# First FFN product of a hybrid decoder layer: a second pair of places for the raw weights of odd units, and shared places for three other tiles

## The chip, the cores and the metric

The kernel runs on one core of one Trainium2 chip. The metric is the time of one launch in microseconds (us), of which the median of several runs is given. One core has five engines that work side by side, each through its own list of instructions in order: TensorE (PE, matmuls, with weight loads shown apart as PEld), VectorE (DVE), ScalarE (ACT), GpSimd (POOL) and SyncE (SP, which only issues transfers). They wait for each other by semaphores. On-chip working memory is divided into tiles of 128 partitions; results of PE appear in banks of 128x512 fp32 numbers, which DVE or ACT then read.

## The reference, cut to what matters

```
h    = rms_norm(x, norm_mix_g)                    # x: 1024 x 1024
proj = h @ w_in                                   # then two attentions, gated and merged
x    = x + merged @ w_out
h2   = rms_norm(x, norm_ffn_g)                    # 1024 x 1024
gu   = h2 @ w_ffn_in                              # 1024 x 5632: gate g and up u, 2816 columns each
x    = x + (silu(gu[..., :2816]) * gu[..., 2816:]) @ w_ffn_down
return rms_norm(x, norm_final_g)
```

All is fp32. The change concerns the line `gu = h2 @ w_ffn_in` with the gate silu(g) * u.

## The kernel before, in words

**Numbers.** A product of two fp32 operands is made of three matmuls. Each operand is held as a pair: a high part (`wh` for weights, `hi` in the code), which ACT makes by a copy in a reduced format (L96), and a low part (`wl`, `lo`), which DVE makes by subtracting the high part from the original (L97). PE multiplies high by high, high by low and low by high.

**Units.** The columns of `w_ffn_in` are worked in 22 units j of 128 columns of g and 128 columns of u. Units 0 and 1 are made plainly (`plain`, in the pool "first"). Units 2 to 21 are made by `up` in the pool "up", with a Winograd form of Strassen's scheme over the pair (g, u) and the two halves of the inner dimension: seven products of half the size instead of eight. Each is 12 matmuls (four blocks of the inner dimension, three matmuls each), 84 in a unit. The left sides come from the raw weights of the unit, two transfers of 512 KB (g and u) that SP issues in `raw_w` (L251) into places named "wr":

- A1: the raw g, split by ACT and DVE.
- S12: u1 + u2 (POOL, L272) and that less g1 (POOL, L273), then split.
- S34: g1 - u1 (L276) and g2 less the second half of S12 (L277), then split.
- A22: u2, the second half of the raw u, split.

In the trace these tiles are all `wh` and `wl`; the raw place is `wr`, the sums are `s`. The right sides (T1 to T4, B11 to B22) are made once, before, and are `hT_t` and `tT` in the trace.

The two raw places of "wr" in the general pool `wpool` are shared by all units, one for g and one for u: the next unit's g can be loaded only when A1, L273, L276 and L277 of this unit have read it.

**Banks and gates.** Each unit takes three of six banks, b1, b2, b3; so a unit's b1 is the b1 of two units before. ACT copies b1 to c1 (L1046), DVE adds (`from_bank`, shown as L978) b2 and c1 to v2; after a second product in b1, ACT takes its sigmoid into sg1 (L1054), and DVE multiplies b1 into sg1 (L978, `sg<-pd,sg`: the last reader of b1). DVE makes v3 (b2 + c1), a2 (b3 + v3) and a1 (b2 + c1); POOL multiplies a1 by sg1 (L1062, the first gate multiply). After the unit's last product DVE makes gt2 (b3 + v2, `gt<-pd,v`), ACT its sigmoid sg2 (L1065), POOL gt2 by sg2 (L1066) and a2 by sg2 (L1067, the second gate multiply). c1, v2, v3, sg1, sg2 and gt2 have one place each in the pool "up"; `a` has two.

**Pairs of units.** The first eight pairs, (2,3) to (16,17), go on into another Strassen scheme for the next product, so each pair's results are combined by four DVE operations into `f1` (L1071, `left_rows`), which are run during the unit after the pair; in the code `todo` carries them there:

```
            vi = from_bank(v2[:], b2, c1)
            if todo:
                with tc.issue_after(vi.ins):
                    left_rows(*todo)
```

POOL's queue then stores `f1` (L1081), and each unit's `a` is stored by POOL's queue too (L1089, L1091, L1094).

**What sets the order.** The order of the instructions on each engine is set at build time by a scheduler that plans with estimated durations and with the places (a new tile of a name waits until the old one in its place has been read); `issue_after` holds an operation back behind another. So a change of places changes the order, too. In the steady order PE runs, from the start of unit n on: A1[:4] x B11 into b1 of n (the start of unit n); A22 x T4 into b2 of n-2; S34[4:] x B22 into b3 of n-2 (the last product of n-2); S12[4:] x T2 into b2 of n; A1[4:] x B21 into b1 of n-1; S12[:4] x T1 into b3 of n and S34[:4] x T3 into b2 of n-1 in turns; then the start of unit n+1. POOL runs in a unit L272 and L273 (of the unit that starts next), L1062, L1066, and then L276, L277, L1067, or, where it has DMAs of a pair to issue, L1067, L276, L277 and the DMAs.

**Around the stage.** Ahead of it lie units 0 and 1, whose last store to `a_dram` (L1007) is in SP's queue ahead of the first loads of the stage. Behind it the next product begins with loads of rows of `a_dram` (L119) into the same raw places of `wpool`.

Of the kernel before, what the change touches and what calls it, by code (L numbers as in the profile page):

```python
# [8 lines left out]
F32 = mybir.dt.float32  # L9
# [6 lines left out]
P = 128  # L16
D = 1024
S = 1024
KT = D // P
# [10 lines left out]
DFF = 2816  # L30
# [17 lines left out]
def layer_kernel(  # L48
# [18 lines left out]
    w_out, w_ffn_in, w_ffn_down = w_out[0], w_ffn_in[0], w_ffn_down[0]  # L67

    def pool_of(name, bufs, side="left"):
        return tc.tile_pool(name=name, bufs=bufs, side=side, reuse_waits="tile")  # L70


    wpool = ctx.enter_context(tc.tile_pool(name="wpool", bufs=2))
# [14 lines left out]
    def nm(s):  # L88
        uid[0] += 1
        return f"{s}_{uid[0]}"  # L90

    def pd():
        return psd.tile([P, HALF], F32, tag="d", name=nm("pd"))

    def split(hi, lo, src):
        nc.scalar.activation(out=hi, in_=src, func=AF.Copy)  # L96
        return nc.vector.tensor_tensor(out=lo, in0=src, in1=hi.bitcast(F32), op=ALU.subtract)  # L97
# [148 lines left out]
    B11, B21 = hT[0][:, :4], hT[0][:, 4:]  # L246
    B12, B22 = hT[1][:, :4], hT[1][:, 4:]

    def raw_w(src):
        t = wpool.tile([P, KT, P], F32, tag="wr", name=nm("wr"), bufs=2)  # L250
        last_w[0] = nc.sync.dma_start(out=t[:], in_=src.rearrange("(k p) c -> p k c", p=P))  # L251
        return t

    def pair_of(raw):

        w = Pair(*[wpool.tile([P, KT, P], F32R, tag="w" + n, name=nm("w" + n), bufs=2) for n in "hl"])
        split(w.hi[:], w.lo[:], raw)
        return w

    def left_side(pool, rg, ru, bufs):  # L260

        def pair(k, tag, bufs):
            return Pair(*[pool.tile([P, k, P], F32R, tag=tag + n, name=nm("w" + n), bufs=bufs) for n in "hl"])

        def fill(w, raw):
            split(w.hi[:], w.lo[:], raw)
            return w

        g1, g2, u1, u2 = rg[:, :4], rg[:, 4:], ru[:, :4], ru[:, 4:]
        S34, A22, A1 = pair(KT, "s34", 1), pair(4, "a22", 2), pair_of(rg[:])  # L270
        s12 = pool.tile([P, KT, P], F32, tag="s", name=nm("s12"), bufs=2)
        nc.gpsimd.tensor_tensor(out=s12[:, :4], in0=u1, in1=u2, op=ALU.add)  # L272
        nc.gpsimd.tensor_tensor(out=s12[:, 4:], in0=s12[:, :4], in1=g1, op=ALU.subtract)  # L273
        S12 = fill(pair(KT, "s12", bufs), s12[:])
        s34 = pool.tile([P, KT, P], F32, tag="s", name=nm("s34"), bufs=2)
        nc.gpsimd.tensor_tensor(out=s34[:, :4], in0=g1, in1=u1, op=ALU.subtract)  # L276
        nc.gpsimd.tensor_tensor(out=s34[:, 4:], in0=g2, in1=s12[:, 4:], op=ALU.subtract)  # L277
        return A1, S12, fill(S34, s34[:]), fill(A22, u2)

    def prod(bank, a, b, first=False):  # L280
        for k in range(4):
            w, m = a[:, k], b[:, k]
            for n, (p, q) in enumerate(((w.hi, m.hi), (w.hi, m.lo), (w.lo, m.hi))):
                last_mm[0] = nc.tensor.matmul(bank[:], p, q, start=first and k == 0 and n == 0,  # L284
                                              stop=k == 3 and n == 2, skip_group_check=True)

    def projections(pool, T, c, dst, dls, sc, hl=False):
# [16 lines left out]

        cc, v2, v3 = [pool.tile([P, HALF], F32, tag=n, name=nm(n), bufs=1) for n in ("cc", "v2", "v3")]
        A1, S12, S34, A22 = left_side(pool, *[raw_w(w_in[:, c0:c0 + P]) for c0 in c], 1)
        b1, b2, b3 = pd(), pd(), pd()

# [73 lines left out]
    with pool_of("foxv", 2) as vpool:  # L382
# [31 lines left out]
        for i in range(NT):  # L414
            load_x()
            hh, c = divmod(i * P, HALF)
# [137 lines left out]
    fpool = f_ctx.__enter__()  # L554
# [288 lines left out]
    for i, (br, dt) in enumerate(merge_order):  # L843
        n = br * KT + dt
# [62 lines left out]
    def rows_of(d):  # L907
        return d.rearrange("n p c -> p n c")
# [5 lines left out]
    with pool_of("wout", 2) as mpool:  # L914
# [13 lines left out]
        for c0 in range(0, D, HALF):  # L928
            ws = []
            for hh in range(2):  # L930
# [12 lines left out]
                if hh == 0:  # L943
                    for k in range(KT):
                        if k % 2 == 0:
                            src = w_out[k * P:(k + 2) * P, c0:c0 + HALF]
# [30 lines left out]
    def from_bank(out, bank, other, op=ALU.add):  # L977
        return nc.vector.tensor_tensor(out=out, in0=bank[:], in1=other[:], op=op)  # L978
# [5 lines left out]
    with pool_of("first", 2) as fpool:  # L984
# [26 lines left out]
        def vec(out, p, q, op=ALU.subtract):  # L1011
            nc.vector.tensor_tensor(out=out[:], in0=p[:], in1=q[:], op=op)
# [21 lines left out]
    with pool_of("up", 1) as fpool:  # L1034

        def tmp(n):
            return fpool.tile([P, HALF], F32, tag=n, name=nm(n), bufs=1)

        def up(j, todo):
            A1, S12, S34, A22 = left_side(fpool, *[raw_w(w_ffn_in[:, c:c + P]) for c in (j * P, DFF + j * P)], 2)  # L1040
            b1, b2, b3 = pd(), pd(), pd()
            a = fpool.tile([P, S], F32, tag="a", name=nm("a"), bufs=2)
            a1, a2 = a[:, :HALF], a[:, HALF:]
            c1, v2, v3, sg1, sg2, gt2 = [tmp(n) for n in ("c1", "v2", "v3", "sg1", "sg2", "gt2")]
            prod(b1, A1[:, :4], B11, True)
            nc.scalar.activation(out=c1[:], in_=b1[:], func=AF.Copy)  # L1046
            prod(b2, S12[:, 4:], T2, True)
# [4 lines that stand above are left out]
            prod(b1, A1[:, 4:], B21)  # L1052

            nc.scalar.activation(out=sg1[:], in_=b1[:], func=AF.Sigmoid)  # L1054
            from_bank(sg1[:], b1, sg1, ALU.mult)
            prod(b2, S34[:, :4], T3)
            from_bank(v3[:], b2, c1)
            prod(b3, S12[:, :4], T1, True)
            from_bank(a2, b3, v3)
            prod(b2, A22, T4)  # L1060
            from_bank(a1, b2, c1)
            nc.gpsimd.tensor_tensor(out=a1, in0=a1, in1=sg1[:], op=ALU.mult)  # L1062
            prod(b3, S34[:, 4:], B22)
            from_bank(gt2[:], b3, v2)
            nc.scalar.activation(out=sg2[:], in_=gt2[:], func=AF.Sigmoid)  # L1065
            nc.gpsimd.tensor_tensor(out=sg2[:], in0=gt2[:], in1=sg2[:], op=ALU.mult)  # L1066
            nc.gpsimd.tensor_tensor(out=a2, in0=a2, in1=sg2[:], op=ALU.mult)  # L1067
            return a[:].rearrange("p (b c) -> p b c", b=2)

        def vec(out, p, q, op=ALU.subtract):  # L1070
            nc.vector.tensor_tensor(out=out, in0=p, in1=q, op=op)  # L1071
            return out

        def left_rows(n, p, q):

            s = f1
            vec(s[:, 0], p[:, 1], q[:, 1], ALU.add)
            vec(s[:, 1], s[:, 0], p[:, 0])
            vec(s[:, 2], p[:, 0], p[:, 1])
            vec(s[:, 3], q[:, 0], s[:, 1])  # L1080
            nc.gpsimd.dma_start(out=rows_of(left_dram[n, 3:7]), in_=s[:])  # L1081

        todo, one = None, None
        for j in range(PLAIN, NFF):
            n, second = divmod(j - 2, 2)
            a = up(j, todo)
            todo = None
            if n >= len(TWO_ROWS):
                nc.gpsimd.dma_start(out=a_dram[j], in_=a.rearrange("p b c -> p (b c)"))  # L1089
            elif second:  # L1090
                nc.gpsimd.dma_start(out=rows_of(left_dram[n, 1:3]), in_=a)  # L1091
                todo = (n, one, a)
            else:
                nc.gpsimd.dma_start(out=left_dram[n, 0], in_=a[:, 0])  # L1094
                one = a
# [5 lines left out]
    with pool_of("down", 1) as fpool:  # L1101
# [79 lines left out]
        A11, A12, A22, S1, S2, S3, S4 = range(7)  # L1181
# [71 lines left out]
```

## Time and profile before

| | us |
|---|---|
| median of 3 runs | 1499.15 |
| lowest and highest | 1495.67, 1503.45 |
| the profiled execution's own time | 1500.5 |
| its span in the profile | 1498.7 |
| units 2 to 21 of the first FFN product | about 863 to 1262 of the span |
| PE busy in the span | 1442.6 |
| DVE, ACT, POOL busy in the span | 952.7, 554.9, 507.9 |

The mean TensorE clock that was granted is 0.996 of full speed. In that stage, 863 to 1262 us, PE is busy for 384.88 of 399.00 us, POOL for 221.86, DVE for 212.44 and ACT for 108.87.

In the rows shown below an operation is named by engine, line, and output<-inputs, with the numbers of the tiles left out; `xN` is a count. A row of the waits gives an engine and operation, what ended its idle time, and then the sum in us, the count and the longest. A row of the timeline begins with the start and the length in us; brackets at its end hold the idle time of the engine ahead of it and what ended it. `pd` is a bank, `s` a POOL sum, `f` is f1, `v` v2 or v3, `sg` sg1 or sg2, `gt` gt2. SPq is the queue in which SP issues transfers.

### The profile page before, as it was taken

How to read it: one execution, taken by the hardware profiler on the slowest of the kernel's cores; microseconds unless marked ns; L12 is line 12 of the kernel's file. 1: busy time of each engine (PE TensorE's matmuls, PEld its weight loads, DVE VectorE, ACT ScalarE, POOL GpSimd, SP SyncE). 2: the span in 40 equal slices, each digit the busy share in tenths (PEclk: the TensorE clock that was granted, in tenths of full speed). 3: DMA queues.
4: the chain of work that ended last, by engine and by line, in shares of the span. 5: the costliest groups of instructions: out<-in, count | busy, mean ns of one | idle time of the engine just before them, and what ended most of it. 6: DMA issues, size and time to landing. Idle time of an engine off the chain costs nothing. (4 is left out here: it accounts for less than half of the span.)

```text
span 1498.7 us, 18274 instructions
## 1 busy us (share of the span) xinstructions
PE 1442.6 (96%) x6824; PEld 1153.7 (77%) x6824; DVE 952.7 (64%) x1336; ACT 554.9 (37%) x832; POOL 507.9 (34%) x446
## 2 busy tenths in 40 slices
PE   6999999999999999999999999999999999999997
PEld 6897888776767666688887788777777777778886
DVE  6483654449988999736528955555554553876556
ACT  5342332226765332355214422222222222633333
POOL 1002434445443311100246165555654554060000
PEclk9999999999999999999999999999999999999999
DMA  8132444565453442175869122333223333976512
GB/s 254 43 106 70 148 155 127 152 186 127 127 150 118 140 156 71 62 241 164 307 216 335 54 91 92 99 105 103 68 82 100 106 112 131 315 256 213 184 39 98
DMA packets 165785, 213.58 MB, mean 143 GB/s; under 512 B 13760, under 2 KB 115136, under 8 KB 165440
## 3 DMA queue, kind: packets, MB, share of 16 engines
q1 hardware_dynamic: 129232, 118.54, 26.0%
q0 software_dynamic: 15200, 55.07, 10.3%
q10 hardware_dynamic: 21264, 38.81, 8.0%
q8 instruction: 54, 0.88, 0.2%
q14 instruction: 35, 0.29, 0.1%
HBM read 146.32 MB, written 66.06 MB: 142 GB/s over the span
## 5 line engine op out<-in xcount | busy, mean ns | idle before, releaser
L284 PE MATMUL pd<-hT_t,wh 128*128 128x512 f32 x856 | 266.2, 392 | 7.8 <-ACT wh L96 6.3
L284 PE MATMUL pd<-tT,wh 128*128 128x512 f32 x768 | 236.6, 390 | 2.7 <-DVE v L978 1.4
L284 PEld LDWEIGHTS pd<-hT_t,wh 128*128 128x128 f32 x856 | 160.4, 188 | 44.5 <-ACT wh L96 9.5
L97 DVE TENSOR_TENSOR wl<-wr,wh 128x1024 fp32r<-128x1024 f32 (+2 forms) x110 | 113.5, 1033 | 108.2 <-ACT wh L96 101.7
L284 PE MATMUL pd<-hT_t,wl 128*128 128x512 f32 x428 | 169.0, 395 | 5.4 <-DVE wl L97 5.2
L284 PEld LDWEIGHTS pd<-tT,wh 128*128 128x128 f32 x768 | 144.1, 188 | 34.4 <-DVE v L978 1.8
L96 ACT ACTIVATE wh<-wr 128x1024 fp32r<-128x1024 f32 (+2 forms) x110 | 95.4, 868 | 201.5 <-DMA wr<-in_w_ffn_in_dram 64.0
L284 PE MATMUL pd<-tT,wl 128*128 128x512 f32 x384 | 148.3, 390 | 0.1
L97 DVE TENSOR_TENSOR wl<-s,wh 128x1024 fp32r<-128x1024 f32 x58 | 82.6, 1425 | 78.6 <-ACT wh L96 78.6
L100 PE MATMUL pf<-hT_t,wh 128*128 128x512 f32 x288 | 114.1, 396 | 1.2 <-ACT wh L96 1.2
L97 DVE TENSOR_TENSOR ol<-raw,oh 128x1024 fp32r<-128x1024 f32 x64 | 86.1, 1360 | 45.9 <-ACT oh L96 42.7
L101 PE MATMUL pf<-hT_t,wh 128*128 128x512 f32 x288 | 114.1, 396 | 0.0
L102 PE MATMUL pf<-hT_t,wl 128*128 128x512 f32 x288 | 113.5, 395 | 0.0
L272 POOL TENSOR_TENSOR s<-wr 128x512 f32<-128x512 f32 x29 | 41.7, 1437 | 210.7 <-DMA wr<-in_w_ffn_in_dram 75.4
L96 ACT ACTIVATE wh<-s 128x1024 fp32r<-128x1024 f32 x58 | 61.4, 1059 | 136.1 <-POOL s L273 114.1
L284 PEld LDWEIGHTS pd<-hT_t,wl 128*128 128x128 f32 x428 | 80.6, 188 | 28.4 <-DVE wl L97 12.0
L96 ACT ACTIVATE oh<-raw 128x1024 fp32r<-128x1024 f32 x64 | 67.2, 1071 | 92.1 <-PE pd L1170 83.3
L1170 PE MATMUL pd<-ol,oh 128*128 128x512 f32 x224 | 87.3, 390 | 1.1 <-DVE ol L97 1.1
L1170 PE MATMUL pd<-oh,ol 128*128 128x512 f32 x224 | 86.5, 389 | 0.0
L925 POOL TENSOR_TENSOR r<-r 128x512 f32<-128x512 f32 x32 | 44.7, 1410 | 121.0 <-DMA r<-in_w_ffn_down_dram 119.6
L1170 PE MATMUL pd<-oh 128*128 128x512 f32 x224 | 85.2, 389 | 0.0
L284 PEld LDWEIGHTS pd<-tT,wl 128*128 128x128 f32 x384 | 72.1, 188 | 15.5 <-DVE wl L97 0.5
(276 smaller groups left out, 3072.5 us busy)
## 6 DMA issues: line engine op xcount, KB each, us to landing
wr<-in_w_in_dram SPq DMA_DIRECT2D x46, 512.0 KB, 4.7
wr<-in_w_ffn_in_dram SPq DMA_DIRECT2D x44, 512.0 KB, 4.5
raw<-left_dram SPq DMA_DIRECT2D x56, 256.0 KB, 4.1
g_dram<-fst ACTq DMA_DIRECT2D x32, 256.0 KB, 2.1
land<-g_dram SPq DMA_DIRECT2D x16, 512.0 KB, 3.6
r<-in_w_ffn_down_dram SPq DMA_DIRECT2D x8, 1024.0 KB, 10.6
right_dram<-r POOLq DMA_DIRECT2D x8, 1024.0 KB, 5.6
left_dram<-f POOLq DMA_DIRECT2D x8, 1024.0 KB, 7.5
```

The source lines that it names most:

```text
L96: nc.scalar.activation(out=hi, in_=src, func=AF.Copy)
L97: return nc.vector.tensor_tensor(out=lo, in0=src, in1=hi.bitcast(F32), op=ALU.subtract)
L100: nc.tensor.matmul(psum, w.hi, m.hi, start=start, stop=False)
L101: nc.tensor.matmul(psum, w.hi, m.lo, start=False, stop=False)
L102: last_mm[0] = nc.tensor.matmul(psum, w.lo, m.hi, start=False, stop=stop)
L272: nc.gpsimd.tensor_tensor(out=s12[:, :4], in0=u1, in1=u2, op=ALU.add)
L284: last_mm[0] = nc.tensor.matmul(bank[:], p, q, start=first and k == 0 and n == 0, stop=k == 3 and n == 2, skip_group_check=True)
L925: nc.gpsimd.tensor_tensor(out=out, in0=p, in1=q, op=ALU.subtract)
L1170: nc.tensor.matmul(bank[:], p, q, start=new and n == 0 and i == 0, stop=n == last and i == 2, skip_group_check=True)
```

## The change

Units with an odd j get a pair of raw places of their own in the pool "up"; those with an even j stay with the pair in `wpool`. So a unit's load waits for the readers of the unit two before it and no longer of the one before. At the same time A22 has one place in this stage instead of two, gt2 is put into the place of v3, and sg2 into that of sg1; these two tiles are now taken behind the unit's last product.

```diff
--- before.py
+++ after.py
@@ -246,8 +246,8 @@
     B11, B21 = hT[0][:, :4], hT[0][:, 4:]
     B12, B22 = hT[1][:, :4], hT[1][:, 4:]
 
-    def raw_w(src):
-        t = wpool.tile([P, KT, P], F32, tag="wr", name=nm("wr"), bufs=2)
+    def raw_w(src, pool=None):
+        t = (pool or wpool).tile([P, KT, P], F32, tag="wr", name=nm("wr"), bufs=2)
         last_w[0] = nc.sync.dma_start(out=t[:], in_=src.rearrange("(k p) c -> p k c", p=P))
         return t
 
@@ -257,7 +257,7 @@
         split(w.hi[:], w.lo[:], raw)
         return w
 
-    def left_side(pool, rg, ru, bufs):
+    def left_side(pool, rg, ru, bufs, a22_bufs=2):
 
         def pair(k, tag, bufs):
             return Pair(*[pool.tile([P, k, P], F32R, tag=tag + n, name=nm("w" + n), bufs=bufs) for n in "hl"])
@@ -267,7 +267,7 @@
             return w
 
         g1, g2, u1, u2 = rg[:, :4], rg[:, 4:], ru[:, :4], ru[:, 4:]
-        S34, A22, A1 = pair(KT, "s34", 1), pair(4, "a22", 2), pair_of(rg[:])
+        S34, A22, A1 = pair(KT, "s34", 1), pair(4, "a22", a22_bufs), pair_of(rg[:])
         s12 = pool.tile([P, KT, P], F32, tag="s", name=nm("s12"), bufs=2)
         nc.gpsimd.tensor_tensor(out=s12[:, :4], in0=u1, in1=u2, op=ALU.add)
         nc.gpsimd.tensor_tensor(out=s12[:, 4:], in0=s12[:, :4], in1=g1, op=ALU.subtract)
@@ -1037,11 +1037,12 @@
             return fpool.tile([P, HALF], F32, tag=n, name=nm(n), bufs=1)
 
         def up(j, todo):
-            A1, S12, S34, A22 = left_side(fpool, *[raw_w(w_ffn_in[:, c:c + P]) for c in (j * P, DFF + j * P)], 2)
+            A1, S12, S34, A22 = left_side(fpool, *[raw_w(w_ffn_in[:, c:c + P], (wpool, fpool)[j % 2])
+                                                   for c in (j * P, DFF + j * P)], 2, 1)
             b1, b2, b3 = pd(), pd(), pd()
             a = fpool.tile([P, S], F32, tag="a", name=nm("a"), bufs=2)
             a1, a2 = a[:, :HALF], a[:, HALF:]
-            c1, v2, v3, sg1, sg2, gt2 = [tmp(n) for n in ("c1", "v2", "v3", "sg1", "sg2", "gt2")]
+            c1, v2, v3, sg1 = [tmp(n) for n in ("c1", "v2", "v3", "sg1")]
             prod(b1, A1[:, :4], B11, True)
             nc.scalar.activation(out=c1[:], in_=b1[:], func=AF.Copy)
             prod(b2, S12[:, 4:], T2, True)
@@ -1061,6 +1062,7 @@
             from_bank(a1, b2, c1)
             nc.gpsimd.tensor_tensor(out=a1, in0=a1, in1=sg1[:], op=ALU.mult)
             prod(b3, S34[:, 4:], B22)
+            gt2, sg2 = tmp("v3"), tmp("sg1")
             from_bank(gt2[:], b3, v2)
             nc.scalar.activation(out=sg2[:], in_=gt2[:], func=AF.Sigmoid)
             nc.gpsimd.tensor_tensor(out=sg2[:], in0=gt2[:], in1=sg2[:], op=ALU.mult)
```

No operation, transfer or size differs. From L1041 on line numbers move by one, from L1064 on by two: the four operations into f1 are L1073 now (L1071 before), sg1's sigmoid L1055 (L1054), c1 L1047 (L1046).

**SP, the loads of units 5 to 7.** The order of SP's transfers stays; what each waits for differs. Before (in brackets the semaphores for which a load waits: Pool and DVE are those of engines, DMAHW those of transfers):

```order
L251 DMA wr_1040_7429<-in_w_ffn_in_dram 128x8x128 [waits DMAHW6_49,Pool_49]
L251 DMA wr_1041_7431<-in_w_ffn_in_dram 128x8x128 [waits DMAHW5_49,Pool_49]
L251 DMA wr_1062_7562<-in_w_ffn_in_dram 128x8x128 [waits DMAHW1_49,DMAHW0_49,Pool_49]
L251 DMA wr_1063_7564<-in_w_ffn_in_dram 128x8x128 [waits DMAHW7_49,DMAHW2_49,Pool_49]
L251 DMA wr_1084_7700<-in_w_ffn_in_dram 128x8x128 [waits DMAHW2_49,Pool_49]
L251 DMA wr_1085_7702<-in_w_ffn_in_dram 128x8x128 [waits DMAHW1_49,Pool_49]
```

and now:

```order
L251 DMA wr_1040_7429<-in_w_ffn_in_dram 128x8x128 [waits DMAHW3_49,DVE_49,Pool_49]
L251 DMA wr_1041_7431<-in_w_ffn_in_dram 128x8x128 [waits DMAHW4_49,DVE_49]
L251 DMA wr_1062_7562<-in_w_ffn_in_dram 128x8x128 [waits DMAHW5_49,DMAHW1_49,Pool_49]
L251 DMA wr_1063_7564<-in_w_ffn_in_dram 128x8x128 [waits DMAHW6_49,DMAHW2_49,DVE_49]
L251 DMA wr_1084_7700<-in_w_ffn_in_dram 128x8x128 [waits DMAHW7_49,Pool_49]
L251 DMA wr_1085_7702<-in_w_ffn_in_dram 128x8x128 [waits DMAHW0_49,DVE_49]
```

The second load of each unit (the raw u) waited for POOL; now it waits for DVE (the split of A22 of the unit two before is its place's last reader).

**DVE, the stretch in which the sums of a pair run.** This is in unit 10, with the f1 sums of units 8 and 9; sg1_1169 is sg1 of unit 10, wl_1153 the low half of S34 of unit 10, and wl_1201 the low half of A1 of unit 12, with which unit 12 starts. Before:

```order
L978 TENSOR_TENSOR v2_1167_8135<-pd_1163_8131,c1_1166_8134 128x512
L1071 TENSOR_TENSOR f1_6754<-a_1121_7862 128x512
L97 TENSOR_TENSOR wl_1153_8109<-s34_1161_8123,wh_1152_8108 128x1024
L1071 TENSOR_TENSOR f1_6754<-a_1121_7862,a_1143_8000 128x512
L1071 TENSOR_TENSOR f1_6754<-f1_6754,a_1121_7862 128x512
L1071 TENSOR_TENSOR f1_6754<-a_1143_8000,f1_6754 128x512
L978 TENSOR_TENSOR sg1_1169_8137<-pd_1162_8130,sg1_1169_8137 128x512
L97 TENSOR_TENSOR wl_1201_8384<-wr_1194_8375,wh_1200_8383 128x1024
L978 TENSOR_TENSOR v3_1168_8136<-pd_1163_8131,c1_1166_8134 128x512
```

and now:

```order
L978 TENSOR_TENSOR v2_1167_8135<-pd_1163_8131,c1_1166_8134 128x512
L1073 TENSOR_TENSOR f1_6754<-a_1121_7862 128x512
L97 TENSOR_TENSOR wl_1153_8109<-s34_1161_8123,wh_1152_8108 128x1024
L1073 TENSOR_TENSOR f1_6754<-a_1121_7862,a_1143_8000 128x512
L1073 TENSOR_TENSOR f1_6754<-f1_6754,a_1121_7862 128x512
L1073 TENSOR_TENSOR f1_6754<-a_1143_8000,f1_6754 128x512
L97 TENSOR_TENSOR wl_1201_8384<-wr_1194_8375,wh_1200_8383 128x1024
L978 TENSOR_TENSOR sg1_1169_8137<-pd_1162_8130,sg1_1169_8137 128x512
L978 TENSOR_TENSOR v3_1168_8136<-pd_1163_8131,c1_1166_8134 128x512
```

The low half of A1 of unit 12 has moved ahead of the multiply of sg1 of unit 10; the four f1 sums stay ahead of both. These two rows have changed places in every unit from 4 on, with f1 sums ahead of them or not.

**ACT, the start of the stage.** wh_983 is S12 of unit 2, wh_976 S34 of unit 2; wh_978 is A22 of unit 2, wh_1002 is A1 of unit 3, and wh_1024 A1 of unit 4. Before:

```order
L96 ACTIVATE wh_978_7031<-wr_975_7027 128x512
L1046 ACTIVATE c1_990_7055<-pd_986_7051 128x512
L96 ACTIVATE wh_983_7040<-s12_982_7037 128x1024
L1054 ACTIVATE sg1_993_7058<-pd_986_7051 128x512
L96 ACTIVATE wh_976_7029<-s34_985_7044 128x1024
L96 ACTIVATE wh_1002_7166<-wr_996_7158 128x1024
L96 ACTIVATE wh_1000_7164<-wr_997_7160 128x512
```

and now:

```order
L96 ACTIVATE wh_978_7031<-wr_975_7027 128x512
L1047 ACTIVATE c1_990_7055<-pd_986_7051 128x512
L96 ACTIVATE wh_1002_7166<-wr_996_7158 128x1024
L96 ACTIVATE wh_983_7040<-s12_982_7037 128x1024
L1055 ACTIVATE sg1_993_7058<-pd_986_7051 128x512
L96 ACTIVATE wh_976_7029<-s34_985_7044 128x1024
L96 ACTIVATE wh_1024_7299<-wr_1018_7291 128x1024
```

A1 of unit 3 has moved ahead of S12 of unit 2, and A1 of unit 4 comes behind S34 of unit 2. PE there has the start of unit 3 inside the products of unit 2's S12 instead of behind them; from about unit 6 on PE's order is that of before.

## The prediction

> **What bounds the kernel now.** I read the page first, then the waits between 863 and 1262 us (the stage that is changed), the chain that ended last, and the timeline of single units in it. Units, products and the order of PE are named as in the section on the kernel before. The first rows are the page's busy time of each engine in the span and the waits of the stage (us in total, times, longest us):
>
> ```profile
> PE 1442.6 (96%) x6824; PEld 1153.7 (77%) x6824; DVE 952.7 (64%) x1336; ACT 554.9 (37%) x832; POOL 507.9 (34%) x446
> ...
> PEld pd L284 <- DVE wl L97: 12.0, 16, 1.0
> PEld pd L284 <- ACT wh L96: 9.5, 8, 1.9
> ...
> POOL s L272 <- DMA wr<-in_w_ffn_in_dram: 75.4, 19, 5.1
> ACT wh L96 <- DMA wr<-in_w_ffn_in_dram: 64.0, 18, 5.1
> SPq L251 <- POOL s L276: 228.2, 17, 15.6
> ```
>
> PE is the bound, so only time in which it stands still can be won. In this stage it stands for the halves of a unit's weights (wh from ACT, wl from DVE). Behind these is the load of wr: POOL and ACT wait for it, and SP holds it back until POOL's L276 and L277 have read the unit before.
>
> How much that is, the chain tells. Its PE pieces begin, when the wait is over, at the third matmul of a unit (start, us, what):
>
> ```profile
> 965.38 19.36 PE pd L284 x84
> ...
> 1066.67 7.79 PE pd L284 x33
> ...
> 1087.74 19.35 PE pd L284 x84
> 1107.09 7.81 PE pd L284 x33
> ...
> 1128.72 9.38 PE pd L284 x33
> ...
> 1211.32 3.70 PE pd L284 x15
> ```
>
> And one such start closely, from the timeline (start, us, engine; in brackets the idle time before it):
>
> ```profile
> 1033.26 0.62 PE L284 MATMUL pd<-tT,wh 128*128 128x512 f32 x2
> ...
> 1043.91 0.39 PE L284 MATMUL pd<-hT_t,wl 128*128 128x512 f32 x1
> 1045.10 0.73 PE L284 MATMUL pd<-hT_t,wh 128*128 128x512 f32 x2 [0.81 <-ACT wh L96]
> 1046.36 0.50 PE L284 MATMUL pd<-hT_t,wl 128*128 128x512 f32 x1 [0.53 <-DVE wl L97]
> ```
>
> From 1033.26 to 1043.91 are 47 steps from matmul to matmul without a wait: 10.65 / 47 = 0.227 us each. A unit of 84 needs 19.07. From 965.38 to 1211.32 are 12 units in 245.94 us, against 228.8: 17.1 lost. Of these, 9.38 - 7.79 = 1.6 in the piece at 1128.72 are matmuls that were slow, not late; they stay. So 15.5 are waits, of two kinds. A unit before whose end DVE runs its four L1071 (a **sum unit**, every other one, eight in all) loses 2.0: 1087.74 - 1066.67 = 21.07. The others (**plain units**) lose little: 1107.09 - 1087.74 = 19.35. The sum unit that ends at 965.38 lies before that stretch and lost 2.0 more.
>
> At the stage's end stands one more wait:
>
> ```profile
> 1248.94 1.23 DVE L97 TENSOR_TENSOR wl<-wr,wh 128x1024 fp32r<-128x1024 f32 x1 [3.52 <-ACT wh L96]
> 1250.09 0.68 DVE L978 TENSOR_TENSOR v<-pd,c 128x512 f32<-128x512 f32 x1
> ...
> 1249.05 0.39 PE L284 MATMUL pd<-hT_t,wl 128*128 128x512 f32 x1
> 1250.82 0.50 PE L284 MATMUL pd<-tT,wh 128*128 128x512 f32 x1 [1.39 <-DVE v L978]
> ```
>
> PE loses 1.77 - 0.23 = 1.5 there and 0.1 by a slow first step. DVE has v3 behind wl of a row of a_dram, the next stage's first load, which came late. All waits that I count: 15.5 + 2.0 + 1.6 = 19.1 us. PEld's two rows and this wait bound them from above, 21.5 + 1.6 = 23.1.
>
> **The change, part by part.** No instruction is added or taken away; bytes and sizes stay.
>
> *Raw places.* The load of a unit now waits for the unit two before it. It is issued about a unit (19 us) ahead, and its 4 to 5 us fit in:
>
> ```profile
> wr<-in_w_ffn_in_dram SPq DMA_DIRECT2D x44, 512.0 KB, 4.5
> L1062 POOL TENSOR_TENSOR a<-a,sg 128x512 f32<-128x512 f32 x19 | 31.4, 1652 | 68.8 <-DVE a L978 68.8
> 1054.91 1.05 ACT L96 ACTIVATE wh<-s 128x1024 fp32r<-128x1024 f32 x1
> 1061.06 1.30 POOL L1067 TENSOR_TENSOR a<-a,sg 128x512 f32<-128x512 f32 x1
> ```
>
> (the page's row of this load, the stage's group of L1062, and two rows of a plain unit, whose last product ends at 1054.9). One place is held longer: u's raw is freed by the split of A22, which now, with one place, waits for the product A22 of the unit before. That ends 24 matmuls (5.4) into a unit; with 1.3 for ACT and DVE and 5.1 for a load the data stand about 12 into it. POOL asks for them behind its second gate multiply: the last product ends 36 matmuls (8.2) in, the multiply 1062.36 - 1054.9 = 7.5 later, 15.7. I cost this at nothing, on nearly 4 us of cover.
>
> *What is late next.* In a sum unit this stands today (unit 9's last product ends at 1033.26; unit 12 starts 48 matmuls on, at 1044.14, if nothing waits):
>
> ```profile
> 1033.45 0.69 DVE L978 TENSOR_TENSOR gt<-pd,v 128x512 f32<-128x512 f32 x1 [1.43 <-PE pd L284]
> 1034.94 1.75 POOL L1066 TENSOR_TENSOR sg<-gt,sg 128x512 f32<-128x512 f32 x1 [1.77 <-ACT sg L1065]
> 1035.46 2.31 DVE L97 TENSOR_TENSOR wl<-s,wh 128x1024 fp32r<-128x1024 f32 x1
> 1036.77 2.15 POOL L1067 TENSOR_TENSOR a<-a,sg 128x512 f32<-128x512 f32 x1
> 1038.95 1.76 DVE L1071 TENSOR_TENSOR f<-a,a 128x512 f32<-128x512 f32 x1 [1.18 <-POOL a L1067]
> 1040.13 1.74 POOL L277 TENSOR_TENSOR s<-wr,s 128x512 f32<-128x512 f32 x1
> 1040.75 1.66 DVE L1071 TENSOR_TENSOR f<-f,a 128x512 f32<-128x512 f32 x1
> 1042.45 0.69 DVE L1071 TENSOR_TENSOR f<-a,f 128x512 f32<-128x512 f32 x1
> 1043.06 0.68 DVE L978 TENSOR_TENSOR sg<-pd,sg 128x512 f32<-128x512 f32 x1
> 1043.44 0.77 POOL L1081 DMA_DIRECT2D left_dram<-f  x1 [0.88 <-DVE f L1071]
> 1043.99 1.06 ACT L96 ACTIVATE wh<-wr 128x1024 fp32r<-128x1024 f32 x1 [4.44 <-DMA wr<-in_w_ffn_in_dram]
> 1045.09 1.22 DVE L97 TENSOR_TENSOR wl<-wr,wh 128x1024 fp32r<-128x1024 f32 x1 [1.34 <-ACT wh L96]
> ```
>
> The last two go: wh of unit 12 is split as soon as A1 of unit 10 is done with, by 1040. But DVE's new order has wl of unit 12 ahead of sg1 of unit 10, and both behind the L1071; and unit 12 starts in the bank from which sg1 reads. So: the last L1071 ends 1043.14; wl 1.22, less the 0.08 by which such rows overlap, to 1044.28; sg1 0.68, to 1044.88; PE at 1044.91. It waits 0.77, and the first step after a wait costs 0.1: 0.87 instead of 2.0, in eight units (the first sum unit had no wait; PE's steady order now begins ahead of it): 7.0. In a plain unit there are no L1071: POOL's multiply ends 7.5 after the last product, wl and sg1 take 1.9, 9.4 in all, and 48 matmuls give 10.9. No wait is left there.
>
> In these rows DVE and POOL take turns: the third L1071 has 1.66 beside L277, the fourth, beside no arithmetic on POOL, 0.69. The Trainium skill, "SBUF — State Buffer", Who interferes with whom, says the same more strictly: a vector instruction with two SBUF inputs and a GpSimd one that reads SBUF exclude each other, and the later fully blocks. By that rule wl of unit 12 may have to stand behind POOL's next L272, and the gain would be gone; that is rival two.
>
> *The stage's start* loses something. ACT now has A1 of the second unit ahead of S12 of the first, and PE needs S12 at once:
>
> ```profile
> 864.26 0.34 SPq L1007 DMA_DIRECT2D a_dram<-a  x1
> 865.94 1.47 SPq L251 DMA_DIRECT2D wr<-in_w_ffn_in_dram  x2
> 866.38 1.05 ACT L96 ACTIVATE wh<-s 128x1024 fp32r<-128x1024 f32 x1
> 869.39 0.61 PE L284 MATMUL pd<-tT,wh 128*128 128x512 f32 x2
> ```
>
> The second unit's load has a free place and goes out behind the store, at 864.65. With 3.9 to 5.1 us to landing A1 is split at 868.6 to 869.8 and S12 1 us later, and PE goes on at 870.7 to 871.9 instead of 869.39: 1.3 to 2.5 lost. I take 1.7, near the lower end, since the first of two loads lands first. With a faster queue it would be nothing.
>
> *The end.* The load from a_dram finds its place a unit earlier; v3 isn't late, and the 1.6 goes.
>
> *Shared places of the temporaries.* gt2 takes v3's place: v3's one reader is DVE itself, and the next v3 comes 48 matmuls (10.9) on, when POOL has long read gt2 (1036.69). sg2 takes sg1's: its sigmoid waits for L1062, which starts 0.9 after the product A22 and takes 1.65; 12 matmuls (2.7) and gt2 cover that. The next sg1 waits for L1067 (1038.92); its own product ends 24 matmuls after 1033.26, at 1038.7 and a tail. Behind it on ACT stands S12 of unit 12, needed at 1053. I take nothing; fewer places can't give a gain. Only an L1067 later than 1042.8 would cost, 1 us a unit for each 1 us.
>
> Sum: 19.1 - 7.0 - 1.7 = 10.4 won. The profiled execution took 1500.5 us, 1.35 above the median of 1499.15: 1490.1, and by the median 1488.7. I say 1488.5.
>
> **The rivals.** *One, all waits in the units go:* sg1 is there in time because the L1071 run faster with less beside them. Against it: POOL's order beside them is the same. 1499.15 - 19.1 + 1.7 = 1481.8. *Two, the sum units stay as they are:* wl of unit 12 waits for one L272 of 1.3; then 2.2 are lost in each, 17.6, and nothing is won: 1499. For it: 2.31 for a wl beside POOL. Against: POOL has L272 behind L1081, which starts 0.4 after wl could. *Three, the change doesn't do what it says:* the loads still land late, because u's raw hangs on A22; the waits stay, 1499 to 1501. Against: the 4 us of cover. *Four, slower:* the shared place of sg. If POOL's second multiply came 5.3 later (behind L276, L277 and one more blocked turn, 1.3 + 1.7 + 2.3), sg1 would be read at 1045.5, 1.4 late in some 18 units: 25 lost for 17.4 won, 1507. It decides from 1 us a unit on. For it: in plain units L276 and L277 stand between the two multiplies. Against: the end is at 7.5 there, 2 us early.
>
> **How the numbers follow.** The forecast has 0.60, rival one 0.10, two 0.14, three 0.08, four 0.08. The forecast's own range is 1485 to 1492 (start 0 to 2.5, sum units 0.5 to 1.2 each). For eight in ten I take 1481 to 1497, which takes in rival one and most of what lies between the forecast and two. The runs before lie 7.8 us apart, so 0.5% (7.5 us) is about what can be told from no change. Faster than 1491.65: 0.60 less 0.05 at its upper edge, and rival one, 0.65. Slower than 1506.6: the larger part of rival four, 0.06. The rest, 0.29, is within 0.5%.
>
> **What would show it.** POOL's L272 and ACT's wh no longer wait for wr (75.4 and 64.0 now). PE stands at a start for DVE's sg, 0.8 long, eight times; sum units take 19.9 us, plain ones 19.1; one stand of 1.3 to 2.5 near 870, released by ACT's wh; none at the stage's end. It is wrong if PE waits for sg in plain units as well, if L272 comes ahead of wl, or if loads still end waits.

## The result, and the profile after

The changed kernel takes 1491.36 us (median of 6 runs, 1487.65 to 1492.55), the kernel before 1499.04 beside it: a ratio of 0.9944, 95% interval 0.9929 to 0.9958, or 7.7 us less. The forecast was 1488.5, 10.5 less. Measured once more later, with four runs, it was 1488.83 against 1501.16, a ratio of 0.9921 (0.9900 to 0.9942), 12.3 less. The gain that was forecast lies between the two gains that were measured. The profiled execution has a span of 1490.8 us, 7.9 less than that of before.

The waits of the changed stage (863 to 1262 us; us in total, times, longest):

```profile
ACT wh L96 <- PE pd L284: 160.6, 57, 8.5
...
PEld pd L284 <- DVE sg L978: 8.5, 8, 1.1
...
ACT wh L96 <- DMA wr<-in_w_ffn_in_dram: 3.3, 2, 2.9
...
PEld pd L284 <- ACT wh L96: 2.3, 1, 2.3
```

POOL's L272 no longer waits for wr (75.4 before), ACT for 3.3 instead of 64.0; ACT's splits now wait for PE, which has to be done with the place. PE stands for sg1 eight times, once for a wh, never for a wl; a wait of 1.1 for c1 at the first unit is as before. The chain that ended last shows the whole of one such stand (start, us, what):

```profile
926.60 27.28 PE pd L284 x119
...
953.96 0.91 ACT wh L96
954.87 0.06 issue
954.93 0.63 ACT sg L1067
955.56 0.07 issue
955.63 1.75 POOL sg L1068
957.38 0.07 issue
957.44 2.16 POOL a L1069
959.63 1.78 DVE f L1073
961.43 1.67 DVE f L1073
...
963.74 0.40 DVE wl L97
964.14 0.73 issue
964.87 0.70 DVE sg L978
965.57 0.04 issue
965.61 27.32 PE pd L284 x119
```

It reads from the unit's second gate multiply (POOL L1069) through the f1 sums and the low half of A1 to sg1, and only then to PE. The period of two units is 965.61 - 926.60 = 39.01 us; before it was 40.3 to 42.0. The same stretch as in the prediction, unit 10, from the timeline:

```profile
1037.70 1.77 DVE L1073 TENSOR_TENSOR f<-a,a 128x512 f32<-128x512 f32 x1 [1.19 <-POOL a L1069]
1038.88 1.73 POOL L277 TENSOR_TENSOR s<-wr,s 128x512 f32<-128x512 f32 x1
1039.50 1.66 DVE L1073 TENSOR_TENSOR f<-f,a 128x512 f32<-128x512 f32 x1
1041.80 1.22 DVE L97 TENSOR_TENSOR wl<-wr,wh 128x1024 fp32r<-128x1024 f32 x1
1042.18 0.77 POOL L1083 DMA_DIRECT2D left_dram<-f  x1 [0.88 <-DVE f L1073]
1042.65 0.39 PE L284 MATMUL pd<-hT_t,wl 128*128 128x512 f32 x1
1042.94 0.68 DVE L978 TENSOR_TENSOR sg<-pd,sg 128x512 f32<-128x512 f32 x1
1042.97 1.29 POOL L272 TENSOR_TENSOR s<-wr 128x512 f32<-128x512 f32 x1
1043.67 0.74 PE L284 MATMUL pd<-hT_t,wh 128*128 128x512 f32 x2 [0.64 <-DVE sg L978]
```

PE starts 1.02 after its last matmul instead of 0.227: 0.80 lost, and 0.11 more by the slow first step. The low half of A1 has its full speed (1.22): POOL's L272 starts only as it ends.

Since both traces hold 6824 matmuls, I can set the start of each against that of the same count before. That gives a ledger, which holds for the one profiled execution of each:

| up to | after less before, us |
|---|---|
| start of the stage, before the first stand | -0.2 |
| behind the stand at 871 | +1.9 |
| first stand for sg1 (926.60) | +2.8 |
| start of unit 10 (1004.66) | +0.2 |
| end of the stage's units (1238) | -12.8 |
| start of the last Strassen products (1281.5) | -11.8 |
| behind the stand in them (1329) | -9.5 |
| behind eight slow matmuls there | -7.9 |

So in these two executions the stage itself won 12.6 us, and 4.9 were given back behind it.

### The profile page after: what moved, and what is told of

The parts are those of the page before. It is cut to its first block, busy times and chain, and to the rows that moved or that the text cites. A ratio compares the mean times of both kernels' runs of the same rounds, so it can differ in the third digit from the quotient of the medians.

```text
span 1490.8 us, 18313 instructions
## 1 busy us (share of the span) xinstructions
PE 1439.4 (97%) x6824; PEld 1155.5 (78%) x6824; DVE 962.8 (65%) x1336; ACT 556.3 (37%) x832; POOL 514.1 (34%) x446
## 4 chain that ended last, share of the span: by engine, by line
PE 76%; DVE 12%; POOL 3%; issue 3%; DMA 3%; ACT 3%; SPq 0%; ACTq 0%; DVEq 0%; POOLq 0%
PE pd L284 30%; PE pd L1172 9%; PE pd L100 6%; PE pd L102 6%; PE pd L101 6%; PE pf L100 3%; PE pf L102 3%; PE pf L101 3%; DVE f L1073 2%; PE pd L662 2%; PE pd L194 1%; PE pd L191 1%; PE pd L190 1%; POOL a L1069 1%; PE pd L611 1%
## 5 line engine op out<-in xcount | busy, mean ns | idle before, releaser
L97 DVE TENSOR_TENSOR wl<-wr,wh 128x1024 fp32r<-128x1024 f32 (+2 forms) x110 | 120.9, 1100 | 106.4 <-ACT wh L96 106.1
L272 POOL TENSOR_TENSOR s<-wr 128x512 f32<-128x512 f32 x29 | 46.6, 1606 | 141.0 <-PE pd L101 65.0
```

## The experiments

Each is the changed kernel with the edit shown, unless said. Ratios are to the kernel before, with 95% intervals; its median was 1499.2 beside the first eight and 1501.2 beside the last four.

### Only the shared places

```diff
-            A1, S12, S34, A22 = left_side(fpool, *[raw_w(w_ffn_in[:, c:c + P], (wpool, fpool)[j % 2])
+            A1, S12, S34, A22 = left_side(fpool, *[raw_w(w_ffn_in[:, c:c + P], None)     # one pair, as before
```

> Only the shared places (A22 one place, gt2 with v3, sg2 with sg1), raw places as before. Theory (the gain comes from the loads): POOL and ACT wait for wr as before (75 and 64 us), PE stands for A1 at the start of the units, time 1499, between 1496 and 1502. Rival (the gain comes from the new order that the shared places bring, not from the loads): 1491 to 1494.

Measured: 1525.89 us, ratio 1.0180 (1.0158 to 1.0202): 27 us slower, which neither theory had. A sum unit, from the timeline (SPq L251 is the next load of u):

```profile
1022.24 0.68 DVE L97 TENSOR_TENSOR wl<-wr,wh 128x512 fp32r<-128x512 f32 x1
1022.95 12.73 SPq L251 DMA_DIRECT2D wr<-in_w_ffn_in_dram  x2
1026.80 1.28 POOL L272 TENSOR_TENSOR s<-wr 128x512 f32<-128x512 f32 x1 [1.83 <-DMA wr<-in_w_ffn_in_dram]
1030.53 1.25 POOL L273 TENSOR_TENSOR s<-s,wr 128x512 f32<-128x512 f32 x1
1031.82 1.06 ACT L96 ACTIVATE wh<-s 128x1024 fp32r<-128x1024 f32 x1 [7.08 <-POOL s L273]
1032.93 0.73 PE L284 MATMUL pd<-tT,wh 128*128 128x512 f32 x2 [3.05 <-ACT wh L96]
```

The first row is the low half of A22: once it is read off, the load of u goes out (1022.95), lands 3.8 later, and L272, L273 and the split follow, with POOL's other work between. PE stands 3.2 us for S12. So the shared places are not free by themselves; with the second raw pair the same row holds back only a load that is not due yet.

### Only the shared places of the gates

As the kernel with only the shared places, but A22 has its two places again:

```diff
-                                                   for c in (j * P, DFF + j * P)], 2, 1)
+                                                   for c in (j * P, DFF + j * P)], 2, 2)
```

> Raw places as before, A22 with two places as before; only gt2 and sg2 share the places of v3 and sg1. Theory: what made the kernel with all shared places and one raw pair slow (1525.9) is A22's one place: the raw u is freed by A22's split, so the next unit's u, L272, L273 and S12 come late (stands of 3.4 us for S12). Without it the time is that of before, 1499, between 1496 and 1503, and PE doesn't wait for S12. Rival (the shared place of sg1 and sg2, which ties sg1's sigmoid to POOL's second gate multiply): it stays slow, 1515 to 1526.

Measured: 1498.85 us, ratio 0.9992 (0.9976 to 1.0008). The 27 us were A22's one place; gt2 and sg2 share at no cost that these runs can tell. The prediction had put that at nothing, and rival four had feared it.

### A second place for g alone

`raw_w` takes a number of places; g stays in `wpool` with two, u gets one in the stage's own pool.

```diff
-            A1, S12, S34, A22 = left_side(fpool, *[raw_w(w_ffn_in[:, c:c + P], (wpool, fpool)[j % 2])
-                                                   for c in (j * P, DFF + j * P)], 2, 1)
+            A1, S12, S34, A22 = left_side(fpool, *[raw_w(w_ffn_in[:, c:c + P], *((fpool, 1) if n == 1 else ()))
+                                                   for n, c in enumerate((j * P, DFF + j * P))], 2, 2)
```

> Two raw places for g, still one for u; A22 keeps two places, gt2 and sg2 share. Theory: a unit begins with A1, which comes from g; S12, which comes from u, is due only 36 matmuls (8.2 us) after it, so u's late load is hidden although POOL's L272 waits for wr again. PE's waits as in the changed kernel, 1491.5, between 1489 and 1494. Rival (both loads matter): PE waits for the halves of S12 inside the units, 1495 to 1499.

Measured: 1497.90 us, ratio 0.9988 (0.9975 to 1.0002). A miss, but not in the units: the stands there are the same eight of 0.80 for sg1, 39.02 us apart. It lost at both ends:

```profile
868.67 1.26 POOL L272 TENSOR_TENSOR s<-wr 128x512 f32<-128x512 f32 x1 [46.03 <-DMA wr<-in_w_ffn_in_dram]
873.96 1.01 PE L284 MATMUL pd<-tT,wh 128*128 128x512 f32 x2 [4.96 <-ACT wh L96]
...
1272.98 0.34 ACTq L136 DMA_DIRECT2D gain<-in_norm_final_g_dram  x1
1273.36 1.57 ACT L1140 ACTIVATE acc<-pd 128x512 f32<-128x512 f32 x3 [5.35 <-issue]
```

The first u goes out only at 864.15, behind SP's store of the last plain unit (L1007), and PE stands 5.1 us. That it goes out so late because its place lies in the stage's own pool, which opens when the pool before is closed, is likely but wasn't tried. At the end ACT has a load of a gain in its queue, which goes out at 1272.98 (1261.70 in the changed kernel); ACT's copies of acc stand behind it, and PE 6.1 us. That this load waits for the memory of the stage's pool is likely, too, and wasn't tried either. For the units a second place for g was enough, with two places for A22.

### The f1 sums behind sg1

```diff
-            vi = from_bank(v2[:], b2, c1)
-            if todo:
-                with tc.issue_after(vi.ins):
-                    left_rows(*todo)
+            from_bank(v2[:], b2, c1)
...
-            from_bank(sg1[:], b1, sg1, ALU.mult)
+            vi = from_bank(sg1[:], b1, sg1, ALU.mult)
+            if todo:
+                with tc.issue_after(vi.ins):
+                    left_rows(*todo)
```

> The changed kernel with the f1 sums put behind the multiply of sg1 on DVE. Theory (PE stands at a start only for sg1, which stands behind the f1 sums): the eight waits of 0.9 us go, 7.3 us in all, 1484, between 1481 and 1487. Rival (the sums then hold up v3, POOL's store of f1 and L272 behind it, so that the wait moves to S12 or to the product of A22): 1488 to 1493.

Measured: 1484.98 us, ratio 0.9909 (0.9889 to 0.9928). No stand for sg1 is left, but a small one for v3, which now has three of the sums ahead of it:

```profile
1043.29 0.68 DVE L978 TENSOR_TENSOR v<-pd,c 128x512 f32<-128x512 f32 x1
...
1043.61 0.39 PE L284 MATMUL pd<-hT_t,wl 128*128 128x512 f32 x1
1044.02 0.74 PE L284 MATMUL pd<-tT,wh 128*128 128x512 f32 x2
```

0.41 - 0.227 = 0.18 and 0.11 for the first step: 0.29 instead of 0.91, eight times, 5 us. By the ledger against the first profile of the changed kernel 4.8 came in the stage, and 3.9 in the last stage, where this profile has a smaller stand and no slow matmuls behind it (below). Against its second profile 4.9 came in the stage and nothing behind it. So the f1 sums were the cause, and a part of the wait only moved, to the product of A22, which goes into the bank that v3 reads, as the rival had it.

### sg1 ahead of the low half of A1

In short (the code also hands the multiply of the unit two before to `left_side`):

```diff
+        with tc.issue_after(sg1_multiply_of_unit_j_minus_2):
             A1 = pair_of(rg[:])
```

> The changed kernel with the multiply of sg1 ahead of the low half of A1 of the unit that starts next; the f1 sums stay ahead of both. Theory (sg1 holds the bank): the start no longer waits, but its third matmul, 0.45 us on, now needs the low half, which is ready 0.6 later than the start was due plus that; 0.3 to 0.5 us lost in each of eight units and not 0.9, so 3.5 to 4.5 us won: 1487.5, between 1485 and 1490. Rival (the low half of A1 is what PE really waits for, sg1 is only the name that came last): no gain, 1491 or more.

Measured: 1503.30 us, ratio 1.0037 (1.0019 to 1.0055): slower, against the theory. The timeline of unit 10 (L277 is here what is L272 elsewhere, L1090 the store of f1):

```profile
1047.56 0.68 DVE L983 TENSOR_TENSOR sg<-pd,sg 128x512 f32<-128x512 f32 x1
1047.94 0.77 POOL L1090 DMA_DIRECT2D left_dram<-f  x1 [0.88 <-DVE f L1080]
1048.16 2.94 DVE L97 TENSOR_TENSOR wl<-wr,wh 128x1024 fp32r<-128x1024 f32 x1
1048.72 1.28 POOL L277 TENSOR_TENSOR s<-wr 128x512 f32<-128x512 f32 x1
1051.15 0.50 PE L289 MATMUL pd<-hT_t,wl 128*128 128x512 f32 x1 [1.91 <-DVE wl L97]
```

The start itself isn't late any more, so the bank was held by sg1, as the theory said. But the low half, 0.6 us later than in the changed kernel, now lies beside POOL's sum and takes 2.94 us instead of 1.22; PE's third matmul loses 2.07. That is the mechanism of the prediction's rival two, brought about by one swap. The Trainium skill, "SBUF — State Buffer", Who interferes with whom, has the two kinds exclude each other, and lets the order of issue decide who waits. By the rows the exclusion agrees; the order doesn't as it stands, since the low half starts 0.56 before the sum and still is the one that waits. Whether the store L1090, which POOL issues from 1047.94 on, gives POOL the turn was not tried.

### S12 of unit 2 ahead of A1 of unit 3

In short, as above:

```diff
+        with tc.issue_after(high_half_of_S12_of_unit_2):      # for unit 3 alone
             A1 = pair_of(rg[:])
```

> The changed kernel with one order more: on ACT the high half of A1 of unit 3 behind that of S12 of unit 2. Theory: the stand of 2.1 us at the start of the stage goes (PE at 869.4 as before); 1489.2, between 1487.5 and 1491. Rival (the stand returns a few products later, where A1 of unit 3 is then late): 1491 to 1492.

Measured: 1489.31 us, ratio 0.9931 (0.9910 to 0.9952). The stand at the start is 0.36 us (0.59 - 0.227) instead of 2.09, and the ledger against the first profile of the changed kernel keeps 1.7 to 1.8 us of it to the end. By time alone it can't be told from the changed kernel.

### The residual's additions spread

```diff
-        banks = product(S2, T2, banks, residual)
+        banks = product(S2, T2, banks, lambda n: n % 2 or residual(n // 2))
-        banks = product(S3, T3, banks)
+        banks = product(S3, T3, banks, lambda n: n % 2 or residual(4 + n // 2))
```

> The changed kernel with POOL's eight additions of the residual (L1151) spread over two products of the last stage, one beside every second of DVE's low halves and not one beside each. Theory: PE's stand of 3.4 us near 1329 (1.2 in the profile of before) is DVE's low halves taking 3.4 us beside POOL's additions and 1.23 without; it shrinks to under 0.5, and 1 to 3.4 us are won: 1489, between 1487 and 1490.5. Rival (the stand is a late load of raw rows): no change, 1491 to 1492.

Measured: 1489.13 us, ratio 0.9937 (0.9917 to 0.9958), the stand 0.93 us. This says nothing: nothing holds POOL back, so it ran the additions at the same points as before, three at once and then as their loads landed. All three edits together:

> All three: the f1 sums behind sg1, S12 of unit 2 ahead of A1 of unit 3, and the residual's additions spread. Theory: 1485.0 with the first alone, less 2.1 at the start, less 1.1 in the last stage (where that kernel stood 1.1): 1481.8, between 1479 and 1484. Rival (the gains overlap, each only moves the next wait): 1484 to 1486.

Measured: 1485.49 us, ratio 0.9904 (0.9884 to 0.9924), with the stand in the last stage at 3.29 us although the same edit is in it. So the stand's size had another reason; the last four runs bear on it.

### The changed kernel again

> The changed kernel once more, for a second profile. Theory: PE's stand in the last stage near 1329 (3.4 us in the first profile, 1.1 to 1.3 or 3.2 to 3.5 in those of other kernels with the same code there) depends on whether one of POOL's residual additions (L1151) lies beside the last low half that DVE makes (3.4 us) or not (1.2); it comes out as one of these two sizes, not between, and the time is 1491 with the large and 1489 with the small one. Rival (it is a property of this kernel's order): 3.4 again, to 0.2.

Measured: 1488.83 us, ratio 0.9921 (0.9900 to 0.9942). The stand is 1.11 us where it was 3.40 in the first profile of the same kernel, so it is no property of the order. DVE's last three low halves and POOL in the first profile:

```profile
1318.89 10.06 DVE L97 TENSOR_TENSOR ol<-raw,oh 128x1024 fp32r<-128x1024 f32 x3
1325.13 2.74 POOL L1151 TENSOR_TENSOR acc<-acc,xr 128x1024 f32<-128x1024 f32 x1
1329.01 0.50 PE L1172 MATMUL pd<-ol,oh 128*128 128x512 f32 x1 [3.24 <-DVE ol L97]
```

and in the second:

```profile
1318.61 7.90 DVE L97 TENSOR_TENSOR ol<-raw,oh 128x1024 fp32r<-128x1024 f32 x3
1325.31 3.46 POOL L1151 TENSOR_TENSOR acc<-acc,xr 128x1024 f32<-128x1024 f32 x1 [0.49 <-DMA xr<-x_dram]
1326.57 0.50 PE L1172 MATMUL pd<-ol,oh 128*128 128x512 f32 x1 [0.95 <-DVE ol L97]
```

In the second POOL waited 0.49 for its load of xr; the last low half went first and POOL's addition took longer. One turn, 2.2 us, goes with when a load lands. Over all profiles with POOL's additions the stand is either 0.4 to 1.3 us (seven, that of before with 1.24 among them) or 3.3 to 3.5 (four). In six of the seven POOL had waited 0.49 to 2.39 for that load of xr, and the last low half took 1.21. In the four it hadn't waited: its addition started 0.02 behind the work before it, some 0.46 ahead of the last low half, which then took 3.36. The seventh, the kernel with a second place for g alone, has its low halves lying otherwise to POOL's additions.

### Without the residual, and with it on DVE

```diff
-        banks = product(S2, T2, banks, residual)
+        banks = product(S2, T2, banks)                    # first kernel: left out
-            nc.gpsimd.tensor_tensor(out=acc[:, t], in0=acc[:, t], in1=xr[:], op=ALU.add)
+            nc.vector.tensor_tensor(out=acc[:, t], in0=acc[:, t], in1=xr[:], op=ALU.add)   # second kernel
```

> The changed kernel without the residual of the last stage: the eight loads of xr and POOL's eight additions (L1151) are left out, so the output lacks x. Theory: the low halves of DVE take 1.23 us each there, PE's stand near 1329 is gone (under 0.3), and with it the slow matmuls behind it: 1487, between 1485 and 1489. Rival (the stand is a late load or an order of DVE's own): the stand stays at 1.2 or 3.4 and the time at 1490 to 1492.

Measured: 1490.97 us, ratio 0.9934 (0.9912 to 0.9956), four runs; its profiled span is 1486.9. Every low half takes 1.23 us:

```profile
1316.99 1.23 DVE L97 TENSOR_TENSOR ol<-raw,oh 128x1024 fp32r<-128x1024 f32 x1 [0.81 <-ACT oh L96]
...
1323.11 1.23 DVE L97 TENSOR_TENSOR ol<-raw,oh 128x1024 fp32r<-128x1024 f32 x1 [0.81 <-ACT oh L96]
```

and PE's stand is gone, so the cause is shown: here POOL's additions and the loads of xr are both left out, and in the next kernel the loads stay and only the additions leave POOL. The time missed its range by 2 us. Between 1262 and 1282 PE lost 1.1 us more than in both profiles of the changed kernel, as it waited 1.5 and not 0.4 for ACT's copies of acc; so this profile ends level with the second one (0.1 apart). Why the copies are later, and whether the 2 us between the two medians of four runs are more than noise (the intervals overlap), stays open.

> The changed kernel with the residual's eight additions on DVE instead of POOL. Theory (two engines that take turns cost more than one that does both): low halves 1.23 us each, eight additions of about 1.2 us between them, DVE in all 9.8 more but 4 x 2.1 less; PE's stand under 1.2; 1488.5, between 1487 and 1491. Rival (DVE now waits for the loads of xr, which POOL waited for before, and PE behind it): a stand of 2 us or more, 1491 to 1494.

Measured: 1489.74 us, ratio 0.9921 (0.9904 to 0.9939). No stand; DVE does both without losing a turn, and waits 2.57 us for a load of xr without holding PE. The edit with the two that had worked:

> The f1 sums behind sg1, S12 of unit 2 ahead of A1 of unit 3, and the residual's additions on DVE. Theory: 1485.0 with the first alone, 2.1 less by the second, and what the third gives (0 to 3): 1482, between 1479.5 and 1484. Rival (DVE's waits for xr give it back): 1484 to 1487.

Measured: 1480.94 us, ratio 0.9866 (0.9845 to 0.9887), 20 us faster than before, and the best of all. Its interval lies apart from both of the changed kernel's. No stand over 1 us is left in its profile behind 845 us.

## Why the prediction was right, and where not

**The loads.** Hidden, as forecast. The split of A22 starts 5.6 us after the unit does (1010.26 - 1004.66; 5.4 forecast), and L272 never waits for u in the units. The cover of nearly 4 us that was named is real: that load of u goes out at 1011.76, and POOL asks for it at 1020.64. Where there is no such cover, with one raw pair, the same A22 costs 27 us.

**The sum units.** 0.87 forecast, 0.91 measured, eight times, in the order that the prediction gave: last sum, low half, sg1, PE. The experiment with the sums behind sg1 shows that they are the cause.

**The plain units.** No wait, as forecast; a sum unit and a plain one take 39.01 us, against 19.9 + 19.1. One row of that sum was too short: the low half and sg1 were put at 1.9 and took 2.9 ahead of unit 11 (1019.46 to 1022.35), as the low half runs beside POOL there and takes 2.29. The start, at 1023.84, was still 1.5 us off.

**The start.** 1.7 forecast, 2.2 measured (2.09 and 0.11), inside the bounds. The load was issued at 864.48 and ACT's split began 4.73 later:

```profile
864.48 4.51 SPq L251 DMA_DIRECT2D wr<-in_w_ffn_in_dram  x4
869.21 1.06 ACT L96 ACTIVATE wh<-wr 128x1024 fp32r<-128x1024 f32 x1 [2.94 <-DMA wr<-in_w_ffn_in_dram]
870.17 1.04 ACT L96 ACTIVATE wh<-s 128x1024 fp32r<-128x1024 f32 x1
871.26 0.73 PE L284 MATMUL pd<-tT,wh 128*128 128x512 f32 x2 [1.93 <-ACT wh L96]
```

The value that was taken, near the lower end, was 0.5 too small.

**The end of the stage.** v3 is not late, and the stand is gone.

**The sum.** 10.4 for the stage; the ledger has 12.6, of which 1.6 are the eight slow matmuls that were inside the stage before and stood elsewhere after. The prediction had taken them as matmuls that stay; they came behind two of the stands that went (1.62 and 0.70 near 1128), so they went, too. Without them the stage came out 0.6 better than forecast.

**What failed** is the step that the sum left out: it took all behind the stage as unchanged. In the profiled execution that part gave back 4.9: 1.0 for a third wait of 0.84 for DVE's acc, where there were two, 2.3 for the turn that DVE lost to POOL, and 1.6 for slow matmuls behind that stand. The first belongs to the change: in all profiles with the second raw pair and the residual DVE has a low half of a raw row ahead of the addition to acc for which PE waits; in the kernel before, and in the two kernels with one raw pair, that addition comes first. Such an order is set at build time. The second and the third differ from one execution to the next: in the other profile of the same kernel the stand is 1.11 long with no slow matmuls behind it, and only 1.0 is given back.

The two measured gains, 7.7 and 12.3, are 4.6 apart; 2.1 of that is the kernel before, whose median was 1499.0 the first time and 1501.2 the second. That the stand's two sizes make up the other 2.5 fits, but isn't shown, as only one execution of each is profiled. So the path was right, and that the total came out so near owes something to luck: a stage that won 2.2 more than the sum and a loss behind it that the sum did not have.

**The rivals.** One: the sums run no faster, the stands stayed. Two: not in the sum units, but by 1.2 us of margin (1042.97 - 1041.80), as the swap showed. Three: no load ends a wait in the units. Four: L1069 ends at 1037.66 in unit 10, before ACT comes to sg1 (1038.38). In the plain units ACT does wait for it (1.27 for unit 9; 11 waits, 15.2 us in all), but sg1 is still there 1.5 us ahead of PE's start, so no time of PE goes there.

## What to carry to other kernels

A second place for a load is worth what the load's wait is worth less the wait that stands next on the same engine; follow the chain one step further than the wait that goes. A place that is shared or taken away is priced by what its reader holds back (here a raw weight and its next load): one place for A22 left no stand with two raw pairs and cost 27 us with one. Where two elementwise engines take turns, the order of two rows on one of them can be worth 2 us, so see what the other engine runs beside a row before it is moved.

## What the runs showed of the hardware

**The clock after a stand.** In 12 of 14 profiles PE ran some eight matmuls at 0.43 us instead of 0.227 shortly after a long stand, 1.6 us lost. The granted clock in one such stretch of the changed kernel (stretch, us, PE, PEld, DVE, ACT and POOL busy, PE's clock, DMA):

```profile
1330.60:1334.00 3.40, 3.40 (x10) 2.63 (x10) 3.40 (x4) 0.00 (x0) 0.78 (x1) 0.55 0.52 158
```

The stretch takes in a little of what lies behind: in the trace's record of the clock it is 0.50 for 3.41 us, from 1330.22 on, and then 1.00. Of the 22 such drops behind 845 us in all profiles, without those at the kernel's end, 21 last 3.41 us and one 6.83. Not every stand brings one: of those of 2.07 to 2.12 us eight of sixteen did, of those of 3 us and more eleven of thirteen, and three times two close together (1.2 to 1.6 and then 0.7), that of the kernel before near 1129 among them. The Trainium skill, "TensorE: Matmul & The Clock Gate", What's actually happening, has a clock at one half or full, set by a window of 3.4 us that runs freely. The two sizes and the length agree. It lets the clock fall after an idle window of about 3.4 us; here stands of 2.1 us were enough.

The traces also show which stands bring it. In each profile all changes of the clock, from the first to the last, lie whole multiples of 3.413 us apart, so they fall on a grid that runs on through the kernel. Cut by this grid, a stretch in which PE doesn't wait has about 15 starts of matmuls. Behind 845 us, in stretches at the full clock, the half clock followed all 14 that had five starts or fewer, 8 of the 29 with six or seven, and none with eight or more. So one and the same stand of 2.1 us costs 1.6 us more or not, by where it lies on the grid, and two shorter stands in one stretch add up.

**The turns of DVE and POOL.** A low half of 128x1024 takes 1.22 to 1.23 us alone and 2.2 to 3.4 beside POOL, with POOL slowed in its turn (1.28 to 2.3 for 128x512), in two stages with quite different work. Which of them comes first is settled by differences of half a microsecond, and so by loads.
